# Residuals and down-product sums of two of three chunks with tokens on partitions, in a two-layer decoder step on one Trainium2 core

## The chip, the cores and the metric

One core of one Trainium2 chip runs the whole step. The metric is the time of one execution in device microseconds: for the kernel before, a median of 2242.09 us over three runs (2241.4 to 2243.4). The profiled execution is one more run, and every duration in this text comes from it. Engines are called as in the profile: PE (TensorE), DVE (VectorE), ACT (ScalarE), POOL (GpSimd), SP (which issues most DMAs).

## The reference

1088 tokens (1024 of a prompt, 64 of a sample) pass two layers. Each layer is a mixer sub-layer and an FFN sub-layer, with RMSNorm ahead of and behind each:

```python
for l in range(2):
    h = rmsnorm(x, g_mix_pre[l])
    if l == 0:   # u, xb, gate_b, gate_c = h @ w_in (1024 -> 2048)
        m = concat([pool_mixer(u), gate_b * conv3(gate_c * xb)]) @ w_out
    else:        # u, v = h @ w_uv (1024 -> 2048); v is normed, mixed over 128 positions
        m = (u * spatial(rmsnorm(v))) @ w_out_c
    x = x + rmsnorm(m, g_mix_post[l])
    h = rmsnorm(x, g_ffn_pre[l])
    f = square(relu(h @ w_up[l])) @ w_down[l]      # 1024 -> 4096 -> 1024
    x = x + rmsnorm(f, g_ffn_post[l])
```

Outputs are x for prompt and sample, the last rows of pool and convolution inputs, and the normed v of the sample.

## The kernel before

**Tiling.** The tokens are three chunks CH: 384, 384 and 320 (256 of the prompt and the 64 of the sample). Every activation lies with features on partitions: a chunk's residual X and its sums ACC are eight tiles of 128 features by n tokens. A product goes to the PE in three passes over halves in the fp32r format (`mm3`, L304): hi·hi at L308, hi·lo at L309, lo·hi at L310, with 128x128 of the weights stationary and the chunk's n tokens moving. So a product in the profile is 128x384 or 128x320; only v of the SGU (L1005) has activations stationary and 256 weight columns moving.

**Weights** (class at L30) stream from DRAM by SP into three raw buffers; ACT rounds them to the high half (L126), DVE subtracts to get the low half (L127), and eight slots hold the result. A slot comes free when its tile is done, and the next is then prepared. In the FFN's last down group the chunks come one after the other, and its weights are listed, loaded and split once for each chunk (`list_ffn`, L276).

**A down product** (`down_unit`, L483, in mixer and SGU; `products`, L953, in the FFN) makes one feature tile of 128 by n tokens; ACT copies the first group's result into ACC, DVE adds later ones (L491, L965).

**A boundary** between two sub-layers (`boundary`, L414) needs the sum over features, that is over partitions: ACT squares each tile and POOL adds the squares up (`sq_add`, L372, L377, L378), DVE transposes and reduces (`rstat`, L344, L348, L350), a small product with `fold` sums over partitions (L353), and six small operations give the reciprocal root (`rsqrt_small`, L330). Then the tiles of ACC are scaled (L424, DVE and POOL in turn), added to X with the post gain (L433), and rounded with the next gain into hh (ACT, L384) and hl (DVE, L385), while a second such sum gives RB, the factor that is multiplied in after the next products (for example L808). The new X is written to DRAM (xd) and read back (`reload_x`) before it is next needed.

**Order.** The code is written in the order of the PE's work; the boundaries are background generators. `pump` advances them between products by a count of steps (E_STEPS in the last block, U_STEPS in the next sub-layer's first products). An engine executes its instructions in the order in which they were written. Each sub-layer takes the chunks in the order 0, 1, 2. Behind a boundary come the leading products of the next sub-layer, chunk by chunk, as its h comes free (`until_ready`). PSUM has six `ps` and two `aux` banks. At the end `out_tiles` (L441) and `final` (L457) transpose x and ACC of each chunk to tokens on partitions (L453, L471) and store them; at the start `begin` (L570) transposes the input tokens (L580).

Of the kernel before, what the change touches and what calls it, by code (L numbers as in the profile page):

```python
# [15 lines left out]
P = 128  # L16
# [4 lines left out]
NC = len(CH)  # L21
PROMPT2 = 256
NSLOT = 8
E_STEPS = 1
FOLD_GAP = 6.0
U_STEPS = 7
F_STEPS = 3
G_STEPS = 3
# [5 lines left out]
class Weights:  # L34
# [18 lines left out]
    def rows(self, w, starts):  # L53
        vs = [w[r:r + P, :].rearrange("p (k n) -> p k n", k=KT) for r in starts]
        lo = self.add((4, P), [v[:, 0:4] for v in vs])
        hi = self.add((4, P), [v[:, 4:8] for v in vs])
        for p in zip(lo, hi):
            self.plan.append((4, list(p)))
# [4 lines left out]

    def down(self, w, k0, nk, m):
        v = w.rearrange("(k p) n -> p k n", p=P)[:, k0:k0 + nk, m * P:(m + 1) * P]
        ids = []
        for q in range(0, nk, 4):
            k = min(4, nk - q)
            ids += self.add((k, P), [v[:, q:q + k]])
        self.plan.append((4, ids))  # L70
# [63 lines left out]
    def done(self, piece, half=None):  # L134
        for s in range(len(piece[1])) if half is None else (half,):
            del self.tiles[piece[1][s]]
            self.prep()
# [3 lines left out]
def decoder_step(ctx: ExitStack, tc: tile.TileContext, I, O):  # L141
# [67 lines left out]
    stage = [a_pool.tile([P, 3 if c < 2 else 2, D], F32, name=f"st{c}", tag=f"acc{c}") for c in range(NC)]  # L209
# [47 lines left out]
    MIDDLE = ([("x", 4), ("hh", 4), ("hl", 4), ("x", 4), ("hh", 4), ("x", 4), ("hh", 4), ("hl", 2)],  # L257
              [[], [0], [1, 2], [3], [4], [5], [6, 7]])
    LAST = ([("x", 4), ("hh", 4), ("hl", 4), ("x", 4), ("hh", 4), ("hl", 4), ("x", 2), ("hh", 4)],
            [[], [0], [1, 2], [3], [4, 5], [6], [7]])  # L260
# [12 lines left out]
    def first_tile(units, u):  # L273
        return sum(k for _, k in units[:u])

    def list_ffn(wu, wd, plan):  # L276
        units, groups = plan
        for j in range(PLAIN):
            W.col(wu, j * P)
        for j in range(PLAIN, NFF, 2):  # L280
            W.pair(wu, j * P)
        for m in range(KT):
            W.down(wd, NFF - KEPT, KEPT, m)
        for g in groups[1:]:
            for _ in range(NC if g is groups[-1] else 1):
                for m in range(KT):
                    W.down(wd, first_tile(units, g[0]), sum(units[u][1] for u in g), m)

    list_ffn(I["w_up"][0], I["w_down"][0], MIDDLE)
# [4 lines left out]
    list_ffn(I["w_up"][1], I["w_down"][1], LAST)  # L294
# [85 lines left out]
    def pre_tile(c, m, g, ss, src=None):  # L380

        n, x, h = CH[c][1], X[c][:, m, :], H[c]
        v = x if src is None else src
        nc.scalar.activation(out=h[0][:, m, :], in_=v, func=AF.Copy, scale=gcol(g + m))  # L384
        nc.vector.scalar_tensor_tensor(out=h[1][:, m, :], in0=v, scalar=gcol(g + m),  # L385
                                       in1=h[0][:, m, :].bitcast(F32), op0=ALU.mult, op1=ALU.subtract)
        if src is not None:
            (nc.scalar.copy if m % 2 else nc.vector.tensor_copy)(out=x, in_=src)
        if ss is not None:
            sq_add(m, x, ss, n)  # L390
# [17 lines left out]

    def reload_x(c):
        n = CH[c][1]  # L410
        X[c] = x_pool.tile([P, KT, n], F32, name=f"x{c}", tag=f"x{c}")
        nc.sync.dma_start(out=X[c].rearrange("p k n -> p (k n)"), in_=xd[c])
# [28 lines left out]
    def out_tiles(c):  # L441

        n, x = CH[c][1], X[c]
        ot = h_pool.tile([P, 3 if c < 2 else 2, D], F32, name=f"ot{c}", tag=f"hl{c}")
        OT[c] = [ot[:, j] for j in range(3 if c < 2 else 2)]
        if c == 2:
            OT[c].append(w_pool.tile([P, D], F32, name="ot_s", tag="w")[0:64])
        for j, o in enumerate(OT[c]):
            r = o.shape[0]
            for g in range(2):  # L450
# [3 lines left out]
                nc.scalar.copy(out=o[:, g * 512:(g + 1) * 512], in_=ps[0:r, :])  # L454
                yield

    def final(c, ss1, gpost):  # L457
# [8 lines left out]
        for j, o in enumerate(OT[c]):  # L466
            r = o.shape[0]
            for g in range(2):
# [3 lines left out]
                oh = o[:, g * 512:(g + 1) * 512]  # L472
# [10 lines left out]
    def down_unit(c, ws, fs, first, ss1=None, steps=0):  # L483
        n, acc = CH[c][1], ACC[c]
        for m in range(KT):
            ps = psum()
            mm3(ps[:, 0:n], [W.get(p, m) + (f[:, 0, :], f[:, 1, :]) for p, f in zip(ws, fs)])
            if first:
                nc.scalar.copy(out=acc[:, m, :], in_=ps[:, 0:n])
            else:  # L490
                nc.vector.tensor_tensor(out=acc[:, m, :], in0=ps[:, 0:n], in1=acc[:, m, :], op=ALU.add)  # L491
            if ss1 is not None:
                sq_add(m, acc[:, m, :], ss1, n)
            if c == NC - 1 and m % 4 == 3:
                for p in ws:
                    W.done(p, m // 4)
            pump(steps)

# [6 lines left out]
    def spare(c, where):  # L505

        shape = [P, 2, CH[c][1]]
        if where == "h":
            return h_pool.tile(shape, F32R, name=f"fh{c}", tag=f"hh{c}")
        if c < 2:  # L510
            return a_pool.tile(shape, F32R, name=f"fa{c}", tag=f"acc{c + 1}")
        return mix_pool.tile(shape, F32R, name="fm", tag="mixa")

    def new_acc(c):
        ACC[c] = a_pool.tile([P, KT, CH[c][1]], F32, name=f"acc{c}", tag=f"acc{c}")
# [3 lines left out]
    def last_block(ws, fs, gpost, gpre, spill=False, vtok=False):  # L519

        for c in range(NC):
            ss1 = tmp()
            down_unit(c, ws, [f[c] for f in fs], False, ss1, E_STEPS if gpre is not None else F_STEPS)
            READY[c] = NORMED[c] = False
            bg.append(boundary(c, ss1, gpost, gpre, spill, vtok) if gpre is not None else final(c, ss1, gpost))

    def up_down(plan, evac, lead_in, gpost, gpre, spill, vtok, before_last=None):
        fs = {}
        for q, (kind, js) in enumerate(plan):
            ws = take(len(js))  # L530
            if kind == "U":
                pairs = list(zip(js, ws))
                spared = plan[-2][1][-1]
                if q == 0 and lead_in:
                    order = [(j, w, c) for c in range(NC) for j, w in pairs]
                else:
                    order = [(j, w, c) for j, w in pairs for c in range(NC)]
                for j, w, c in order:
                    f = None
                    if q == 0 and lead_in:  # L540
                        if j == 0:
                            while len(bg) > NC - 1 - c:
                                pump(1)
                            f = spare(c, "acc")
                    if j == spared:
                        f = spare(c, "h")
                    fs.setdefault(j, {})[c] = evac(j, c, w, f)
                    if c == NC - 1:
                        W.done(w)
                    pump(U_STEPS)  # L550
                if q == 0:
                    drain()
            elif kind == "D":
                first = js[0] == 0
                for c in range(NC):
                    if first:
                        new_acc(c)
                    down_unit(c, ws, [fs[j][c] for j in js], first)
                for j in js:
                    fs.pop(j)  # L560
            else:
                if before_last:
                    before_last()
                if gpre is None:
                    for c in range(NC):
                        bg.append(out_tiles(c))
                last_block(ws, [fs.pop(j) for j in js], gpost, gpre, spill, vtok)


    def begin(c):  # L570
# [3 lines left out]
        direct = c == 0  # L574
        if direct:
            new_h(c)
        def turn(ps, j, m):
            v = staged(c, j)[:, m * P:(m + 1) * P]
            r = v.shape[0]
            nc.tensor.transpose(ps[:, j * P:j * P + r], v, ident[0:r, 0:r])  # L580

        if direct:
            pss = [psum() if m < 6 else aux() for m in range(KT)]
            for j in range(3):
                for m in range(KT):
                    turn(pss[m], j, m)
# [571 lines left out]
```

## Time and profile before

| | |
|---|---|
| median of three runs | 2242.09 us (2241.4 to 2243.4) |
| the profiled execution's own time | 2240.17 us |
| its span, first to last instruction | 2238.4 us |
| mean granted clock of the PE | 0.982 |
| busy share of the span | PE 96%, DVE 59%, ACT 34%, POOL 10% |
| PE instructions, DVE, ACT, POOL | 13119, 2479, 1450, 229 |

The page gives busy times, 40 slices of the span, DMA queues, the chain that ended last and the costliest groups of instructions. A share over the whole span mixes stretches with different limits, so windows of single stretches, the waits of one engine and its timeline are read beside it. In a row of the timeline the first number is the start in us, the second the length, and in square brackets the idle time before it with what ended it. Starts of PE rows are measured, their ends modelled, so the distance of starts is what a product costs in a stream.

### The profile page before, as it was taken

How to read it: one execution, taken by the hardware profiler on the slowest of the kernel's cores; microseconds unless marked ns; L12 is line 12 of the kernel's file. 1: busy time of each engine (PE TensorE's matmuls, PEld its weight loads, DVE VectorE, ACT ScalarE, POOL GpSimd, SP SyncE). 2: the span in 40 equal slices, each digit the busy share in tenths (PEclk: the TensorE clock that was granted, in tenths of full speed). 3: DMA queues.
4: the chain of work that ended last, by engine and by line, in shares of the span. 5: the costliest groups of instructions: out<-in, count | busy, mean ns of one | idle time of the engine just before them, and what ended most of it. 6: DMA issues, size and time to landing. Idle time of an engine off the chain costs nothing. (4 is left out here: it accounts for less than half of the span.)

```text
span 2238.4 us, 33370 instructions
## 1 busy us (share of the span) xinstructions
PE 2149.3 (96%) x13119; PEld 2127.2 (95%) x13119; DVE 1331.0 (59%) x2479; ACT 752.6 (34%) x1450; POOL 231.7 (10%) x229
## 2 busy tenths in 40 slices
PE   7999997999999999999789999889999999999998
PEld 7999996999999999999789999879999999999997
DVE  6746677966666334445973545688666663343256
ACT  5331133533335212113442221435333361121045
POOL 3100054000000000001530000640000000000002
PEclk9999998999999999999899999989999999999999
DMA  6211222433334223225321113224333352142053
GB/s 203 84 40 49 67 96 90 137 109 98 102 106 159 62 79 107 83 78 172 111 93 57 56 41 113 67 84 137 104 106 94 106 164 89 45 129 63 28 188 121
DMA packets 252608, 219.07 MB, mean 98 GB/s; under 512 B 11744, under 2 KB 241628, under 8 KB 249372
## 3 DMA queue, kind: packets, MB, share of 16 engines
q1 hardware_dynamic: 224076, 165.11, 23.9%
q10 hardware_dynamic: 28376, 51.84, 6.5%
q8 instruction: 103, 1.69, 0.3%
q14 instruction: 53, 0.43, 0.1%
HBM read 160.74 MB, written 56.28 MB: 97 GB/s over the span
## 5 line engine op out<-in xcount | busy, mean ns | idle before, releaser
L309 PE MATMUL ps<-hl,w 128*128 128x384 f32 (+1 forms) x1696 | 559.0, 330 | 10.7 <-DVE hl L385 10.5
L308 PE MATMUL ps<-hh,w 128*128 128x384 f32 (+1 forms) x1696 | 557.0, 331 | 11.9 <-ACT hh L384 10.9
L310 PE MATMUL ps<-hh,w 128*128 128x384 f32 (+1 forms) x1696 | 557.5, 329 | 4.8 <-DVE w L127 4.8
L126 ACT CAST w<-raw 128x512 fp32r<-128x512 f32 (+1 forms) x468 | 277.5, 598 | 758.6 <-PE ps L310 686.0
L310 PE MATMUL ps<-F,w 128*128 128x384 f32 (+1 forms) x1440 | 473.3, 329 | 11.7 <-DVE w L127 11.7
L308 PE MATMUL ps<-F,w 128*128 128x384 f32 (+1 forms) x1440 | 472.9, 328 | 0.0
L309 PE MATMUL ps<-F,w 128*128 128x384 f32 (+1 forms) x1440 | 472.1, 328 | 0.0
L127 DVE TENSOR_TENSOR w<-raw,w 128x512 fp32r<-128x512 f32 (+1 forms) x468 | 317.6, 683 | 188.6 <-ACT w L126 186.6
L309 PEld LDWEIGHTS ps<-hl,w 128*128 128x128 f32 x1696 | 324.3, 191 | 16.8 <-DVE hl L385 16.7
L965 DVE TENSOR_TENSOR acc<-ps,acc 128x384 f32<-128x384 f32 (+1 forms) x288 | 152.4, 533 | 315.1 <-PE ps L310 314.9
L308 PEld LDWEIGHTS ps<-hh,w 128*128 128x128 f32 x1696 | 324.2, 192 | 13.9 <-ACT hh L384 12.2
L310 PEld LDWEIGHTS ps<-hh,w 128*128 128x128 f32 x1696 | 324.3, 191 | 5.7 <-DVE w L127 5.4
L310 PEld LDWEIGHTS ps<-F,w 128*128 128x128 f32 x1440 | 272.6, 189 | 13.0 <-DVE w L127 13.0
L378 POOL TENSOR_TENSOR tmp<-tmp 128x384 f32<-128x384 f32 (+1 forms) x105 | 108.4, 1033 | 1686.6 <-ACT tmp L377 1685.2
L308 PEld LDWEIGHTS ps<-F,w 128*128 128x128 f32 x1440 | 272.6, 189 | 0.2 <-ACT w L126 0.2
L309 PEld LDWEIGHTS ps<-F,w 128*128 128x128 f32 x1440 | 272.5, 189 | 0.0
L809 ACT ACTIVATE f<-f 128x384 f32<-128x384 f32 (+1 forms) x192 | 96.4, 506 | 178.2 <-DVE f L808 176.7
L308 PE MATMUL ps<-f,w 128*128 128x384 f32 (+1 forms) x432 | 141.3, 329 | 4.4 <-ACT f L501 4.4
L890 DVE TENSOR_TENSOR f<-ps,f 128x384 f32<-128x384 f32 x182 | 100.9, 554 | 74.3 <-PE ps L310 68.7
L310 PE MATMUL ps<-f,w 128*128 128x384 f32 (+1 forms) x432 | 141.9, 328 | 0.0
L309 PE MATMUL ps<-f,w 128*128 128x384 f32 (+1 forms) x432 | 141.6, 328 | 0.0
L309 PE MATMUL ps<-t,w 128*128 128x384 f32 x312 | 104.6, 335 | 0.0
(202 smaller groups left out, 2673.5 us busy)
## 6 DMA issues: line engine op xcount, KB each, us to landing
raw<-in_w_down_dram SPq DMA_DIRECT2D x144, 256.0 KB, 2.9
raw<-in_w_up_dram SPq DMA_DIRECT2D x128, 256.0 KB, 3.0
fd<-f ACTq DMA_DIRECT2D x120, 192.0 KB, 2.0
F<-fd SPq DMA_DIRECT2D x28, 768.0 KB, 7.2
xd<-x ACTq DMA_DIRECT2D x8, 1536.0 KB, 7.2
x<-xd SPq DMA_DIRECT2D x8, 1536.0 KB, 8.3
fd<-f ACTq DMA_DIRECT2D x60, 160.0 KB, 1.9
F<-fd SPq DMA_DIRECT2D x14, 640.0 KB, 5.2
```

What stands on the lines that cost most here:

```text
L126: nc.scalar.copy(out=wt[:, 0], in_=raw)
L127: nc.vector.tensor_tensor(out=wt[:, 1], in0=raw, in1=wt[:, 0].bitcast(F32), op=ALU.subtract)
L308: nc.tensor.matmul(out, lhsT=lh, rhs=rh, start=(j == 0), stop=False)
L309: nc.tensor.matmul(out, lhsT=lh, rhs=rl, start=False, stop=False)
L310: nc.tensor.matmul(out, lhsT=ll, rhs=rh, start=False, stop=(j == last))
L378: nc.gpsimd.tensor_tensor(out=ss[:, 0:n], in0=ss[:, 0:n], in1=t[:, 0:n], op=ALU.add)
L809: nc.scalar.activation(out=o, in_=o, func=AF.Square)
L890: tt(out=out, in0=ps, in1=v, op=ALU.add)
L965: tt(out=acc[:, m, :], in0=ps, in1=acc[:, m, :], op=ALU.add)
```

## The change

For chunks 0 and 1 the residual X and the sums ACC now have tokens on partitions: three blocks of 128 tokens by 1024 features. Chunk 2 stays with features on partitions. Each sub-layer's down products, boundary and leading products take the chunks in the order 2, 0, 1 (ORD).

- *Down products* of chunks 0 and 1 (`down_tok`) have 128 tokens of the activation stationary and 512 columns of the weights moving, so a group makes six results of 128x512 and not eight of 128x384. A down group takes both halves of the columns, each over all chunks, and its four weight tiles come free together. The last group's weights are listed once.
- *Boundaries* of chunks 0 and 1 (`boundary_tok`) sum squares along the free dimension on ACT; per block of 128 tokens DVE makes one product with reciprocal root and post gain (the gains are spread over the partitions by a DMA) and one addition over 1024 features, then ACT squares x and writes normed x into ACC (`normed`). There is no fold product and no factor RB: `plainly`, `times` and `squared` leave it out for these chunks.
- *`arrive`* transposes normed ACC of a chunk by 24 products into all eight PSUM banks, and ACT and DVE make hh and hl from there with the gain.
- X of chunks 0 and 1 starts as the input tokens and is stored at the end without transposes; `sums` (the FFN's Strassen sums) is computed from hh and hl. E_STEPS goes from 1 to 3, and x is reloaded one down group earlier in the FFN.

The core of the diff:

```diff
+ORD = (2, 0, 1)
-E_STEPS = 1
+E_STEPS = 3
...
+    def normed(c, j, v, junk, out):
+        ms = sm.tile([P, 1], F32, name="ms", tag="ms")
+        nc.scalar.activation(out=junk, in_=v, func=AF.Square, scale=1.0 / 32.0, accum_out=ms)
+        _, r = rsqrt_small(ms, 1)
+        nc.scalar.activation(out=out, in_=v, func=AF.Copy, scale=r)
...
+    def boundary_tok(c, last):
...
+        for j in range(3):
+            ms = sm.tile([P, 1], F32, name="ms", tag="ms")
+            nc.vector.tensor_tensor(out=ms, in0=SS1[c][:, j, 0:1], in1=SS1[c][:, j, 1:2], op=ALU.add)
+            _, r = rsqrt_small(ms, 1)
+            nc.vector.scalar_tensor_tensor(out=acc[:, j], in0=acc[:, j], scalar=r, in1=GB[0], op0=ALU.mult, op1=ALU.mult)
+            nc.vector.tensor_tensor(out=x[:, j], in0=x[:, j], in1=acc[:, j], op=ALU.add)
...
+            yield
+            normed(c, j, x[:, j], acc[:, j], acc[:, j])
+            nc.scalar.dma_start(out=xd[c][:, j * D:(j + 1) * D], in_=x[:, j])
+            yield
+        TOK[c] = True
+
+    def arrive(c, g):
+        while not TOK.get(c):
+            pump(1, True)
+        new_h(c)
+        n = CH[c][1]
+        pss = [psum() if m < 6 else aux() for m in range(KT)]
+        for m in range(KT):
+            for j in range(3):
+                nc.tensor.transpose(pss[m][:, j * P:(j + 1) * P], ACC[c][:, j, m * P:(m + 1) * P], ident)
+        for m in range(KT):
+            v, (hh, hl) = pss[m][:, 0:n], H[c]
+            nc.scalar.activation(out=hh[:, m, :], in_=v, func=AF.Copy, scale=gcol(g + m))
+            nc.vector.scalar_tensor_tensor(out=hl[:, m, :], in0=v, scalar=gcol(g + m),
+                                           in1=hh[:, m, :].bitcast(F32), op0=ALU.mult, op1=ALU.subtract)
+
+    def sum_tok(c, j, h, v, first, last):
+        acc = ACC[c][:, j, h * 512:(h + 1) * 512]
...
+            nc.vector.tensor_tensor(out=acc, in0=v, in1=acc, op=ALU.add)
+        if last:
+            junk = fslot(c, F32).rearrange("p a n -> p (a n)")[:, 0:512]
+            nc.scalar.activation(out=junk, in_=acc, func=AF.Square, scale=1.0 / 32.0, accum_out=SS1[c][:, j, h:h + 1])
+
+    def down_tok(c, j, h, p, right, first, last=False):
+        t = slice(j * P, (j + 1) * P)
...
+            terms.append((fh[:, t], fl[:, t], w[:, 0].rearrange("p a n -> p (a n)"), w[:, 1].rearrange("p a n -> p (a n)")))
+        mm3(ps, terms)
+        sum_tok(c, j, h, ps, first, last)
...
+    def last_block(ws, right, gpost, gpre, spill, vtok):
+        for c in ORD:
...
+            for j, h in order:
+                down_tok(c, j, h, ws[h], right[c], False, True)
+                if c == ORD[-1] and j == 2:
+                    W.done(ws[h])
+                pump(E_STEPS)
+            bg.append(boundary_tok(c, gpre is None))
...
-        for c in range(NC):
-            n, ss1 = CH[c][1], tmp()
-            for m in range(KT):
-                w = take(1)[0]
-                products(len(GROUPS) - 1, w, m, c)
-                W.done(w)
-                sq_add(m, ACC[c][:, m, :], ss1, n)
-                pump(G_STEPS)
+        last_block(take(2), unit(len(UNITS) - 1), gpost, gpre, spill, vtok)
```

The order of instructions, at the first boundary (mixer to FFN of layer 0). On PE of the kernel before, the fold product (L353) of chunk 0's second statistics stands inside the FFN's leading products of that chunk (hh_3073, hl_3074):

```order
L309 MATMUL ps<-hl_3074,w 128x384
L310 MATMUL ps<-hh_3073,w 128x384
L353 MATMUL aux<-red,fold 128x12
L308 MATMUL ps<-hh_3073,w 128x384
L309 MATMUL ps<-hl_3074,w 128x384
```

In the change the feature chunk goes first, and its second fold (L339 now) stands inside the last block, between the down products of chunk 1 (w moving, 512 columns; f and fh hold the mixer's results):

```order
L294 MATMUL ps<-w,fh_2642 128x512
L295 MATMUL ps<-w,fh_2642 128x512
L296 MATMUL ps<-w,fh_2642 128x512
L339 MATMUL aux<-red,fold 128x10
L294 MATMUL ps<-w,f_2140 128x512
```

So what waits behind this fold moved from leading products to down products.

On PE of the change, at the end of chunk 2's leading products (hh_2937) and ahead of chunk 0's (hh_3463); acc_1340 is chunk 0's normed ACC:

```order
L296 MATMUL ps<-hh_2937,w 128x320
L454 MATMUL ps<-ident,acc_1340 128x128 x5
L454 MATMUL aux<-ident,acc_1340 128x128
L454 MATMUL ps<-ident,acc_1340 128x128
L454 MATMUL aux<-ident,acc_1340 128x128
L454 MATMUL ps<-ident,acc_1340 128x128 x6
L454 MATMUL aux<-ident,acc_1340 128x128 x2
L454 MATMUL ps<-ident,acc_1340 128x128 x6
L454 MATMUL aux<-ident,acc_1340 128x128 x2
L294 MATMUL ps<-hh_3463,w 128x384
```

Twenty-four transposes, eight for each block of 128 tokens, came in between the leading products of two chunks; before, these followed each other directly.

On DVE of the kernel before, between the leading products of chunk 0 and those of chunk 1 (f_3382 is the reciprocal root spread out by a transpose, x_2815 chunk 1's residual):

```order
L357 STREAM_TRANSPOSE f_3382<-y 128x384
L424 TENSOR_TENSOR acc_991<-acc_991,f_3382 128x384 x2
L433 SCALAR_TENSOR_TENSOR x_2815<-acc_991,gains,x_2815 128x384 x3
L385 SCALAR_TENSOR_TENSOR hl_3462<-x_2815,gains,hh_3461 128x384
L424 TENSOR_TENSOR acc_991<-acc_991,f_3382 128x384
L385 SCALAR_TENSOR_TENSOR hl_3462<-x_2815,gains,hh_3461 128x384
```

On DVE of the change, from chunk 0's last block of 128 tokens (acc_1340, x_2711) to chunk 1's first (acc_1365, x_2713):

```order
L433 SCALAR_TENSOR_TENSOR acc_1340<-acc_1340,y,gb 128x1024
L434 TENSOR_TENSOR x_2711<-x_2711,acc_1340 128x1024
L431 TENSOR_TENSOR ms<-ss_3019 128x1
L322 TENSOR_SCALAR v<-ms 128x1 x2
L323 RECIPROCAL y<-y 128x1
L324 TENSOR_TENSOR t<-v,y 128x1
...
L327 TENSOR_TENSOR y<-t,y 128x1
L433 SCALAR_TENSOR_TENSOR acc_1365<-acc_1365,y,gb 128x1024
L434 TENSOR_TENSOR x_2713<-x_2713,acc_1365 128x1024
L458 SCALAR_TENSOR_TENSOR hl_3464<-ps,gains,hh_3463 128x384
```

Scales, x updates and hl by feature tile (L424, L433, L385 of before) gave way to operations over 1024 features and small ones; chunk 0's first hl (L458) now stands behind chunk 1's first block.

## Rows read from the trace of the kernel before

**Rows 1.** The page, busy time by engine: us, share of the span, instructions.
```profile
PE 2149.3 (96%) x13119; PEld 2127.2 (95%) x13119; DVE 1331.0 (59%) x2479; ACT 752.6 (34%) x1450; POOL 231.7 (10%) x229
```
**Rows 2.** The page, the chain that ended last, by engine.
```profile
PE 42%; DVE 4%; DMA 1%; issue 1%; ACT 0%; POOL 0%; DVEq 0%; ACTq 0%; SPq 0%; POOLq 0%
```
**Rows 3.** Windows: length, busy PE, PEld, DVE, ACT, POOL, clock, DMA share, GB/s.
```profile
320.00:420.00 100.00, 82.82 (x445) 78.30 (x444) 87.36 (x160) 47.33 (x101) 41.51 (x36) 0.91 0.31 105
1060.00:1160.00 100.00, 78.14 (x497) 75.24 (x496) 91.24 (x167) 47.04 (x115) 51.04 (x46) 0.90 0.34 114
1430.00:1515.00 85.00, 66.54 (x350) 62.44 (x349) 70.61 (x125) 37.37 (x80) 43.25 (x38) 0.88 0.29 99
1700.00:1800.00 100.00, 100.00 (x613) 100.00 (x612) 67.11 (x115) 38.20 (x70) 0.00 (x0) 1.00 0.31 96
```
**Rows 4.** Waits of PE: line, releaser, us in total, times, longest.
```profile
PE aux L353 <- DVE red L350: 21.2, 9, 6.0
PE ps L310 <- DVE w L127: 16.4, 7, 4.9
PE ps L308 <- ACT hh L384: 10.9, 4, 3.8
...
PE ps L308 <- ACT f L501: 4.4, 2, 2.4
```
**Rows 5.** Timeline of PE at the third boundary.
```profile
1454.63 0.57 PE L353 MATMUL aux<-red,fold 128*128 128x12 f32 x2 [5.98 <-DVE red L350]
...
1456.47 0.52 PE L309 MATMUL ps<-hl,w 128*128 128x384 f32 x1
1456.79 0.52 PE L310 MATMUL ps<-hh,w 128*128 128x384 f32 x1
```
**Rows 6.** Timeline of PE, first and last starts of unbroken stretches of one width.
```profile
1204.93 0.28 PE L308 MATMUL ps<-w,hh 128*128 128x256 f32 x1
...
1209.97 0.28 PE L308 MATMUL ps<-w,hh 128*128 128x256 f32 x1
...
1959.68 0.33 PE L308 MATMUL ps<-F,w 128*128 128x384 f32 x1
...
1965.40 0.31 PE L308 MATMUL ps<-F,w 128*128 128x320 f32 x1
...
1968.91 0.34 PE L308 MATMUL ps<-F,w 128*128 128x384 f32 x1
```
**Rows 7.** Timeline of PE, transposes at the end of the program.
```profile
2163.97 2.79 PE L453 MATMUL ps<-ident,x 128*128 128x128 f32 x12 [2.83 <-DMA x<-xd]
...
2206.39 1.03 PE L471 MATMUL ps<-ident,acc 128*128 128x128 f32 x8
```
**Rows 8.** Groups by line and shape: busy us, mean ns | idle before, releaser.
```profile
L948 DVE TENSOR_TENSOR F<-F 128x1536 fp32r<-128x1536 f32 x28 | 49.2, 1756 | 28.5 <-ACT F L947 28.4
L127 DVE TENSOR_TENSOR w<-rawsum,w 128x512 fp32r<-128x512 f32 x52 | 35.9, 691 | 4.1
L385 DVE SCALAR_TENSOR_TENSOR hl<-x,gains,hh 128x320 fp32r<-128x320 f32 x32 | 27.2, 860 | 0.0
L433 DVE SCALAR_TENSOR_TENSOR x<-acc,gains,x 128x320 f32<-128x320 f32 x24 | 18.4, 794 | 0.0
L424 DVE TENSOR_TENSOR acc<-acc,f 128x320 f32<-128x320 f32 x12 | 7.9, 679 | 0.0
```
**Rows 9.** Groups by line and shape: small operations of the reciprocal root.
```profile
L338 DVE TENSOR_TENSOR t<-v,y 128x12 f32<-128x12 f32 x16 | 3.3, 206 | 0.4
L335 ACT ACTIVATE y<-aux,eps_t 128x12 f32<-128x12 f32 x16 | 4.3, 269 | 20.9 <-PE aux L353 20.8
```
**Rows 10.** Timeline of PE, the last product of the program.
```profile
2221.80 0.31 PE L310 MATMUL ps<-F,w 128*128 128x320 f32 x1
```
**Rows 11.** DMA issues of the last 14 us: count, KB each, median us to landing.
```profile
out_dram<-ot SPq DMA_DIRECT2D x9, 256.0 KB, 2.4
```

More of the change, by code (lines that the diff above doesn't have):

```diff
@@ L132, in get, with tile, done @@
         return t[:, 0, k % per, :], t[:, 1, k % per, :]
[L134 to L137, printed above, removed]
+    def tile(self, piece, k):
+        return self.tiles[piece[1][k]]
+    def done(self, piece):
+        for i in piece[1]:
+            self.free(i)
 @with_exitstack
@@ L271, in list_plan, with first_tile, list_ffn @@
                 W.rows(wd, [j * P for j in ts_])
[L273 to L277, printed above, removed]
+    def first_tile(u):
+        return sum(k for _, k in UNITS[:u])
+    def list_ffn(wu, wd):
         for j in range(PLAIN):
@@ L281, in list_ffn @@
             W.pair(wu, j * P)
-        for m in range(KT):
[L283 to L289, printed above, removed]
+        W.rows(wd, [k * P for k in range(NFF - KEPT, NFF)])
+        for u, (_, k) in enumerate(UNITS):
+            W.rows(wd, [(first_tile(u) + q) * P for q in range(k)])
+    list_ffn(I["w_up"][0], I["w_down"][0])
     for cb in range(4):
@@ new lines, in down_feat @@
+    def down_feat(c, m, p, right, first, ss1=None):
+        n, acc = CH[c][1], ACC[c]
+        ps = psum()[:, 0:n]
+        terms = []
+        for k, (fh, fl) in enumerate(right):
+            w = W.tile(p, k)
+            terms.append((w[:, 0, m % 4, :], w[:, 1, m % 4, :], fh, fl))
+        mm3(ps, terms)
+        if first:
+            nc.scalar.copy(out=acc[:, m, :], in_=ps)
+        else:
+            nc.vector.tensor_tensor(out=acc[:, m, :], in0=ps, in1=acc[:, m, :], op=ALU.add)
+        if ss1 is not None:
+            sq_add(m, acc[:, m, :], ss1, n)
@@ new lines, in down_group @@
+    def down_group(ws, right, first, after=None):
+        for h in range(2):
+            for c in ORD:
+                if first and h == 0:
+                    new_acc(c)
+                if c == 2:
+                    for m in range(4 * h, 4 * h + 4):
+                        down_feat(c, m, ws[h], right[c], first)
+                else:
+                    for j in range(3):
+                        down_tok(c, j, h, ws[h], right[c], first)
+                if h and after:
+                    after(c)
+            W.done(ws[h])
@@ L481, in final @@
                 yield
[L483 to L497, printed above, removed]
     def split_f(c, src, f=None):
@@ L517, in decoder_step, with rights @@
     fd = [dram.tile([P, NFF, n], F32, name=f"fd{c}") for c, (off, n) in enumerate(CH)]
[L519 to L527 removed]
+    def rights(fs):
+        return {c: [(f[c][:, 0, :], f[c][:, 1, :]) for f in fs] for c in range(NC)}
@@ L1000, in decoder_step @@
+        for u in range(-1, len(UNITS) - 1):
+            load(u + 1)
+            if u == len(UNITS) - 2:
+                for c in ORD:
+                    reload_x(c)
+            down_group(take(2), unit(u), u < 0, lambda c: split(u + 1, c))
+        post_gain("g_ffn_post", layer)
+        if gpre is None:
+            bg.append(out_tiles(2))
+        last_block(take(2), unit(len(UNITS) - 1), gpost, gpre, spill, vtok)
     ffn(0, G_MIX_PRE + 8, True, True)
```

380 lines of the change are left out of this document (178 added, 202 removed).

## Prediction

> **What bounds the kernel now.** I read the page first: TensorE (PE) is busy 96% of the span, VectorE (DVE) 59% [rows 1]; the chain that ended last is PE by far, with DVE next at 4% [rows 2]. So the time is the PE's stream plus the places where it breaks. The windows show where [rows 3]. In a steady stretch of the FFN the PE is busy 100.00 of 100 us at clock 1.00; what the other engines do there costs nothing. At the three boundaries where norms must be finished before the next products (mixer to FFN 320–420, FFN to SGU 1060–1160, SGU to FFN 1430–1515) the PE is busy 82.82 of 100, 78.14 of 100 and 66.54 of 85 us, at clocks 0.91, 0.90 and 0.88. Idle time plus what the clock takes (length times one minus the clock) is 17.2 + 9.0 = 26, 21.9 + 10 = 32 and 18.5 + 10.2 = 29 us: **87 us in all**. Next, who is waited for [rows 4]: the fold product of the statistics waits for DVE (21.2 us), products for a split weight tile (16.4), for the first normed tiles hh (10.9), and for a split FFN activation f (4.4). What follows a wait is slow too: after the wait of 5.98 at 1454.63 products of 384 columns start 0.32 us apart, against 0.173 in the steady stretch; that is the 1.2 GHz level after idling [rows 5, 6].
>
> **The change, part by part.** The sum is made against the profiled execution, 2240.2 us (span 2238.4 and 1.8 outside it); the median of the runs shown is 1.9 above that, and I add it at the end. About 4.5 us (0.2%) is what a measurement here can tell from no change.
>
> 1. *Wide down products.* For two chunks 3840 products of 384 columns become 2880 of 512: the same columns, 960 fewer products. In unbroken stretches 33 products of 384 take 5.72 us, 24 of 320 take 3.51 and 42 of 256 take 5.04 [rows 6], i.e. 173.3, 146.3 and 120.0 ns each. All three are columns/2.4 GHz + 13.3 ns, so 512 should take 226.7, and each product that goes saves 13.3 ns: **−12.8 us**. The bound on the poor side is no saving (512 at 4/3 of 173.3 = 231.1). The products of 256 already have activations stationary and weights moving, so that exchange costs nothing by itself. The Trainium skill, TensorE: Matmul & The Clock Gate, section "Wait — 56ns, not 53.3ns?", gives a fixed cost of about 2.5 ns per warm product, not 13.3; by it this term would be an estimated −2.4 us. The three pitches here disagree with it, and the trace decides.
>
> 2. *Transposes.* Three boundaries get 2 × 24 each (+144); 96 at the output go. Eight in the stream took 1.03 us, about 0.107 each without the tail that the model adds to the last; twelve after a wait took 2.79, about 0.21 each [rows 7]. 48 × 0.107 = **+5 us**; with all new ones at the slow level 144 × 0.21 − 96 × 0.107 = +20. I keep +5, since the first sixteen of an arrival can run in time that the PE would idle. The Trainium skill, same page, "Part 4: PE-mode transpose", says that the fast clock does not engage for transposes, which would be the +20; the eight at 0.107 speak against it.
>
> 3. *Boundaries.* What goes for two chunks: a scale, an update of x and an hl from SBUF per feature tile, each 0.68 to 0.86 us on DVE even at 320 columns [rows 8], and the POOL sums behind the folds. What comes: per 128 tokens two DVE operations of 1024 and some fourteen small ones, two ACT passes of 1024, later hl from PSUM. A two-input operation of 1024 is not in the trace: two of 512 are 1.38, two thirds of 1536 is 1.17, and the line between 0.691 and 1.756 gives 1.22 [rows 8]. I take that for ACT's passes too. Small operations take 0.2 in a dependent row, the square root 0.27 [rows 9].
> The order, with time from the token chunks' first last-block unit: twelve units of 12 products of 512, 2.72 us each, 32.6. The feature chunk's first fold stands behind the fourth unit (10.9), its second behind the tenth (27.2), but between them DVE has 4 scales of 0.679, 8 updates of 0.794, 8 hl of 0.860, five sums of 0.69 and 2.7 of small operations, transpose and reduce: 22.1. So the second fold can run at 33.0, and a **wait of 5.8 us stays there**; two more go to the clock after it. The units end at 40.4. The feature chunk's leading products, 96 × 0.146 = 14.0, cover to 54.4. The squares of the token chunks want an f slot that the mixer's and SGU's operands hold until the last unit, so chunk 0's chain starts at about 40. Per 128 tokens it is 0.2 + 0.27 + 1.2 and 2 × 1.22 (post norm and x), 1.22 (square), 0.27 + 1.2 and 1.22 (copy): 8.0, three times 24, ready at 64.4. The PE idles about 10, and the last transposes, first evictions and slow level cost about 3 over the two arrivals. That is 5.8 + 2 + 10 + 3 = **21 us lost per boundary** whose operands sit in f slots, and some 18 at the FFN-to-SGU one, which has no such slots, and where most of the waits for weight tiles (16.4 us in seven [rows 4]) fall: the last down group's weights are now prepared once (8 tiles) and not once per chunk. 87 falls to 60: **−27 us**. The bounds: 12 per boundary (chains that overlap) is −51; no gain at all is 0.
>
> 4. *FFN hand-over.* The two waits for f behind the up products (4.4 in two [rows 4]) go, since the feature chunk's first four units of two terms (24 × 0.146 = 3.5 us) now cover the split of chunk 0's last tile: **−5 us** with the slow level after them; uncovered, 0.
>
> 5. *Start and end.* Chunks 0 and 1 are normed before they are transposed, so the first products come later, but no wait for their statistics follows, and DVE and POOL have less to do in the first mixer phase: **−1.5**, between +4 and −5. At the end x is reloaded one group earlier, so the wait of 2.83 goes [rows 7], −3. Behind the last product, ended at about 2222.1 of 2238.4 [rows 10], that is 16.3 us, stand now a sum (0.7), a square (0.8), two chains of 1.5 + 2.4 in row on DVE and a store of 512 KB, between one and two times the 2.4 of 256 KB [rows 11]: 11.7 to 14.1. I take 14.3 with hand-overs, **−2**, together −5.
>
> 6. *At nothing:* sums into ACC (6 of 512 for 8 of 384) lie beside a PE at 100% with DVE at 67% [rows 3]; without that cover they would move a few tenths per group. POOL loses most of its work, off the chain. SP issues the gains' broadcast ahead of the twelve units, which it has to land; the reloads of x now stand ahead of weight tiles one group earlier, and what is late next if they hold these up is the group before the last. Weight slots come free four at once and not one: hidden by half a group, 23 us, against 4 tiles of 0.69 on DVE.
>
> Sum: −12.8 + 5 − 27 − 5 − 1.5 − 5 = −46.3, so 2193.9 in a profiled run and **2196 us** as a median.
>
> **Rivals.** *Boundaries don't gain* (term 3 zero): the wait for chunk 0's chain takes the place of the waits for folds, hh and weights. For it: DVE stays busiest there, and the chain changes between ACT and DVE four times per 128 tokens. Against: less DVE work in all, and 14 us of cover. Time 2196 + 27 = **2223**.
> *Slower:* chunk 0's chain is stretched because its small DVE operations each stand behind other DVE work (weight splits, relu of the feature chunk, chunk 1's chain): at 0.69 behind every one of some forty the 24 us become 52, the idle 38 and not 10 at each boundary. That is +84, so **2280**; it decides from 17 us more per boundary on (46.3 + 4.5, by three). Against it: in the DVE order chunk 1's first multiply stands behind chunk 0's third.
> *Wide products save nothing* (231.1 each): 2196 + 12.8 = **2209**. For it: no product of 512 is in the trace. Against: three pitches on one line. The Trainium skill's rule in term 1 would land close by.
> That the change doesn't do what it says is excluded by the order of instructions: PE has 928 fewer matmuls, POOL 138 fewer operations.
>
> **How the numbers follow.** Forecast 0.60, its own range 2170 to 2207; boundaries without gain 0.20; wide products without gain 0.10; slower 0.10. The first three are faster by over 0.2% but for a tail of the second, 0.03; so faster 0.87, same 0.03, slower 0.10. Range: 2170 (boundaries at 12 each) to 2232 (the second rival with the start at its bad end); outside are the slower case and a little below.
>
> **What would show it.** In the profile after: products of 512 columns 0.227 apart in the steady FFN; a PE wait of 5 to 6 us at a boundary's second fold; then a PE idle of 8 to 11 us ahead of the last transposes of chunk 0, named as waiting for ACT's normed copy; dips of the clock at the same three places, shallower; no wait for f or x. I am wrong if chunk 0's arrival idles the PE for over 16 us, if wide products stand 0.231 or more apart, or if waits for weight tiles appear in the steady FFN.

## The result and the profile after

The changed kernel takes 2180.41 us (median of 4 runs, 2178.21 to 2182.16), the kernel before 2242.74 (4 runs): a ratio of 0.9722, interval 0.9705 to 0.9738, so 62 us less. The profiled execution has a span of 2177.0 us against 2238.4.

Of the page, busy time by engine and the chain that ended last, which answer to [rows 1, 2]:

```profile
PE 2113.6 (97%) x12175; PEld 1985.4 (91%) x12175; DVE 1275.7 (59%) x2521; ACT 689.5 (32%) x1302; POOL 73.0 (3%) x93
...
PE 91%; DVE 6%; DMA 1%; ACT 1%; issue 1%; SPq 0%; POOL 0%; ACTq 0%; DVEq 0%; POOLq 0%
```

The chain of before is followed back only to 1180 us, which is why its shares in [rows 2] add up to 48%; its 42% and the 91% here can't be set against each other.

The same windows as [rows 3], moved with the shorter program, the second one 15 us longer (three boundaries, a steady stretch of the FFN):

```profile
300.00:400.00 100.00, 88.66 (x476) 81.88 (x475) 81.71 (x203) 57.02 (x122) 11.88 (x11) 0.93 0.30 103
1050.00:1165.00 115.00, 103.85 (x717) 96.80 (x716) 76.66 (x202) 57.72 (x144) 12.42 (x13) 0.94 0.25 87
1390.00:1475.00 85.00, 73.55 (x403) 68.09 (x402) 70.69 (x178) 53.93 (x116) 11.06 (x11) 0.92 0.33 115
1600.00:1700.00 100.00, 100.00 (x611) 100.00 (x610) 67.55 (x116) 29.65 (x51) 0.00 (x0) 1.00 0.33 102
```

The three boundaries still dip, less than before; POOL's 41 to 51 us there are down to 11 or 12. The PE's waits, against [rows 4]:

```profile
PE ps L454 <- ACT acc L417: 18.6, 9, 4.2
PE aux L339 <- DVE red L336: 14.7, 3, 5.1
...
PE ps L294 <- DVE hl L458: 5.7, 7, 3.3
```

Nothing waits for weight tiles or x any more, and f stands at 0.6 us. Two waits are left at every boundary: the second fold (L339), and the transposes (L454) for a chunk's normed copy (L417). Of the latter's 18.6 us, 15.5 lie at the boundaries and 3.1 at the start of the program.

**Where the 61.4 us of span went.** I set each stretch of the PE against what its products would take at columns/2.4 GHz + 13.3 ns, and call the rest lost. The boundary rows cover 320 to 420, 1060 to 1200 and 1430 to 1515 us before and the first three windows above after; a single row holds to within 1 us, since a stretch can be cut in more than one place. The starts of all products, stretch by stretch, give:

| stretch | lost before | lost after | forecast of the difference |
|---|---|---|---|
| start (0–100) | 28.7 | 27.6 | −1.5 |
| mixer to FFN | 29.1 | 19.9 | −5 |
| up to down products, twice | 6.5 | 0.9 | −5 |
| FFN to SGU | 37.6 | 20.4 | −14 |
| SGU to FFN | 29.8 | 19.0 | −8 |
| end | 22.4 | 15.4 | −5 |
| elsewhere | 13.2 | 13.3 | 0 |
| sum | 167.3 | 116.5 | −38.5 |
| the products themselves | 2071.1 | 2060.5 | −7.8 |

### The profile page after: what moved, and what is told of

The parts are those of the page before. It is cut to its first block, busy times and chain, and to the rows that moved or that the text cites. A ratio compares the mean times of both kernels' runs of the same rounds, so it can differ in the third digit from the quotient of the medians.

```text
span 2177.0 us, 30946 instructions
## 1 busy us (share of the span) xinstructions
PE 2113.6 (97%) x12175; PEld 1985.4 (91%) x12175; DVE 1275.7 (59%) x2521; ACT 689.5 (32%) x1302; POOL 73.0 (3%) x93
## 4 chain that ended last, share of the span: by engine, by line
PE 91%; DVE 6%; DMA 1%; ACT 1%; issue 1%; SPq 0%; POOL 0%; ACTq 0%; DVEq 0%; POOLq 0%
PE ps L294 30%; PE ps L296 30%; PE ps L295 30%; DVE hl L370 1%; DVE x L554 1%; DVE acc L467 1%; PE aux L1157 1%; DVE x L434 1%; DVE acc L433 1%; DMA x<-in_x_prompt_dram 1%; DVE w L117 0%; DVE acc L545 0%; DVE hl L458 0%; DMA F<-fd 0%; DMA raw<-in_w_down_dram 0%
## 5 line engine op out<-in xcount | busy, mean ns | idle before, releaser
L295 PE MATMUL ps<-hl,w 128*128 128x384 f32 (+1 forms) x1696 | 550.1, 325 | 0.1
L116 ACT CAST w<-raw 128x512 fp32r<-128x512 f32 x404 | 248.9, 621 | 649.3 <-PE ps L296 572.8
L117 DVE TENSOR_TENSOR w<-raw,w 128x512 fp32r<-128x512 f32 x404 | 275.2, 688 | 147.8 <-ACT w L116 144.1
L467 DVE TENSOR_TENSOR acc<-ps,acc 128x512 f32<-128x512 f32 x240 | 164.7, 688 | 263.3 <-PE ps L296 263.2
L294 PE MATMUL ps<-w,F 128*128 128x512 f32 x720 | 281.7, 391 | 0.0
L296 PE MATMUL ps<-w,F 128*128 128x512 f32 x720 | 281.3, 391 | 0.0
L295 PE MATMUL ps<-w,F 128*128 128x512 f32 x720 | 281.2, 391 | 0.0
L296 PEld LDWEIGHTS ps<-w,F 128*128 128x128 f32 x720 | 135.7, 189 | 28.6
L295 PEld LDWEIGHTS ps<-w,F 128*128 128x128 f32 x720 | 135.7, 189 | 27.2
L294 PEld LDWEIGHTS ps<-w,F 128*128 128x128 f32 x720 | 135.7, 189 | 27.1
L294 PE MATMUL ps<-F,w 128*128 128x320 f32 x480 | 148.3, 309 | 0.0
L296 PE MATMUL ps<-F,w 128*128 128x320 f32 x480 | 148.3, 309 | 0.0
L295 PE MATMUL ps<-F,w 128*128 128x320 f32 x480 | 148.3, 309 | 0.0
L493 DVE TENSOR_TENSOR acc<-ps,acc 128x320 f32<-128x320 f32 x160 | 76.9, 489 | 105.2 <-PE ps L296 104.1
L1029 ACT CAST F<-F 128x1536 fp32r<-128x1536 f32 (+3 forms) x48 | 64.1, 1335 | 206.4 <-DMA F<-fd 198.1
```

What stands on the lines that cost most here:

```text
L116: nc.scalar.copy(out=wt[:, 0], in_=raw)
L117: nc.vector.tensor_tensor(out=wt[:, 1], in0=raw, in1=wt[:, 0].bitcast(F32), op=ALU.subtract)
L294: nc.tensor.matmul(out, lhsT=lh, rhs=rh, start=(j == 0), stop=False)
L295: nc.tensor.matmul(out, lhsT=lh, rhs=rl, start=False, stop=False)
L296: nc.tensor.matmul(out, lhsT=ll, rhs=rh, start=False, stop=(j == last))
L467: nc.vector.tensor_tensor(out=acc, in0=v, in1=acc, op=ALU.add)
```

## The experiments

Each was timed in three rounds beside the kernel before; ratios are to that kernel, and the change stands at 0.9722 (0.9705 to 0.9738).

**1. Narrow products again.** In `down_tok`:

```diff
-        mm3(ps, terms)
+        for q in range(2):
+            s = slice(q * 256, q * 256 + 256)
+            mm3(ps[:, s], [(fh_, fl_, wh[:, s], wl[:, s]) for fh_, fl_, wh, wl in terms])
```

> The changed kernel, but each down product of 512 weight columns is made as two of 256: the same columns, 2880 more products. Theory (13.3 ns for each product on top of its columns): 2880 x 13.3 ns = 38 us more than the change, about 2219 us, and products of 256 start 0.120 us apart. Rival A (a fixed 2.5 ns for each product): 7 us more, about 2188. Rival B (columns alone count, and the gain of the change came from the boundaries): no difference, 2180.

Measured: 2212.89 us, ratio 0.9876 (0.986 to 0.9893); the span is 2211.7, 34.7 more than the change's. Timelines of the PE in steady down products: of the change (the first of 72 wide products, and what follows the last), then of the experiment (144 of 256):

```profile
1931.68 0.39 PE L294 MATMUL ps<-w,F 128*128 128x512 f32 x1
...
1948.02 0.30 PE L294 MATMUL ps<-F,w 128*128 128x320 f32 x1
```

```profile
1933.40 0.28 PE L294 MATMUL ps<-w,F 128*128 128x256 f32 x1
...
1950.67 0.31 PE L294 MATMUL ps<-F,w 128*128 128x320 f32 x1
```

That is 16.34 / 72 = 226.9 ns and 17.27 / 144 = 119.9 ns, both on the line from [rows 6] (226.7 and 120.0). The products account for 38 us more, and some 3 less are lost, most of it in the waits for the fold (11.3 us and not 14.7): a unit of 24 narrow products takes 2.88 us and not 2.72, so DVE has more time up to the fold. The theory stands, and with it the sign and size of term 1: the 960 products that went are worth 12.8 us. The Trainium skill's 2.5 ns (TensorE: Matmul & The Clock Gate, "Wait — 56ns, not 53.3ns?") would have made this experiment an estimated 7 us; with these fp32r products it was 35.

**2. The second fold later.** `rstat` of the second statistics yields a gap of 14.0 us and not FOLD_GAP, so the fold product stands behind the last block:

```diff
-        yield FOLD_GAP
+        yield gap
```

> The changed kernel, but the fold product of the feature chunk's second statistics is written 14 us of PE work behind its reduce and not 6, so behind the last block. Theory (the three waits of 4.8 to 5.1 us on it are lost time, with the slow clock after them): they go, 14 to 20 us less than the change, 2161 to 2167. Rival (the waits lie ahead of work that is not ready anyway): the waits for chunk 0's normed tiles grow by as much, and the time stays within 3 us of 2180.

Measured: 2174.31 us, ratio 0.9704 (0.969 to 0.9719). Waits of PE, and its timeline at the first boundary:

```profile
PE ps L454 <- ACT acc L417: 26.9, 12, 3.9
...
342.73 1.28 PE L454 MATMUL ps<-ident,acc 128*128 128x128 f32 x6 [2.49 <-ACT acc L417]
...
348.33 1.54 PE L454 MATMUL ps<-ident,acc 128*128 128x128 f32 x6 [3.89 <-ACT acc L417]
...
353.72 1.54 PE L454 MATMUL ps<-ident,acc 128*128 128x128 f32 x6 [3.42 <-ACT acc L417]
```

All three waits for the fold are gone, but those for the normed tiles grew from 18.6 to 26.9: of 14.7 us some 6 are kept by median, under 5 in the spans (2172.4), 4 by the ratios, whose intervals just overlap. Neither forecast holds; the truth lies nearer the rival: what ends a boundary is chunk 0's chain.

**3. A tile of its own for the squares.** In `sum_tok`:

```diff
-            junk = fslot(c, F32).rearrange("p a n -> p (a n)")[:, 0:512]
+            junk = JUNK[0]
```

> The changed kernel, but the squares of the token chunks' sums have a tile of their own for their unused output and do not wait for an f slot. Theory of the prediction (chunk 0's chain starts late because its squares wait for slots held by mixer and SGU operands): the chain starts some 8 us earlier at those two boundaries, the waits for normed tiles there (5.8 us each) go, 8 to 14 us less, 2166 to 2172. Rival (the chain starts late because its first multiply stands in DVE's order behind the sum of chunk 1's last unit): squares come earlier, the multiply does not, and the time stays within 3 us of 2180.

Measured: 2179.72 us, ratio 0.9732 (0.9718 to 0.9747): no difference from the change. DVE of the experiment at the first boundary, chunk 1's last sum and chunk 0's first multiply:

```profile
333.84 0.69 DVE L468 TENSOR_TENSOR acc<-ps,acc 128x512 f32<-128x512 f32 x1 [0.27 <-PE ps L296]
...
336.58 1.28 DVE L434 SCALAR_TENSOR_TENSOR acc<-acc,y,gb 128x1024 f32<-128x1024 f32 x1
```

Chunk 0's squares ran from 297.34 on and not from 307.44 as in the change, and yet its first multiply came at 336.58 (334.68 in the change), still behind chunk 1's last sum. My reason for the late chain was wrong in this order of work, though its time was right.

**4. The last down group's weights three times.** `list_ffn` lists the last unit once for each chunk again, and `last_block` takes and releases two pieces per chunk:

```diff
-            W.rows(wd, [(first_tile(u) + q) * P for q in range(k)])
+            for _ in range(NC if u == len(UNITS) - 1 else 1):
+                W.rows(wd, [(first_tile(u) + q) * P for q in range(k)])
```

> The changed kernel, but the weights of the FFN's last down group are loaded and split once for each chunk, as before the change. Theory (the boundary from FFN to SGU gained 17 us and the two others 9 and 11 because the repeated weights went): 6 to 10 us more at that boundary, and 0 to 4 at the end of the program, 2186 to 2194, with waits for weight tiles in both places. Rival (the repeated weights cost nothing, the larger gain has another reason): within 3 us of 2180.

Measured: 2180.56 us, ratio 0.9733 (0.9719 to 0.9748). The rival holds: at the FFN-to-SGU boundary two waits for weights appear (2.1 and 1.9 us), the wait for the fold there goes, and the sum is nothing; at the end of the program no wait for weights appears. In the new layout the single loading, which I gave a part of the FFN-to-SGU gain, is worth nothing.

**5. The pace of before.** E_STEPS = 1 in the changed kernel.

> The changed kernel, but the background work of a boundary is advanced by one step behind each product unit of the last block, as before the change, and not by three. Theory (the gain came from layout, not from the pace): the second fold then falls behind the last block as in the run with the late fold, and chunk 0's chain starts behind it, so 2172 to 2184. Rival (the pace gave much of the gain): 2195 or more, with waits for the feature chunk's own tiles.

Measured: 2189.75 us, ratio 0.9777 (0.9762 to 0.9791), between the two. The wait of PE for the normed copies, and its last rows:

```profile
PE ps L454 <- ACT acc L417: 34.7, 13, 6.1
```

```profile
2159.82 0.39 PE L296 MATMUL ps<-w,F 128*128 128x512 f32 x1
...
2160.19 2.82 PE L591 MATMUL ps<-ident,acc 128*128 128x128 f32 x24
```

As in 2 the second fold falls behind the last block and costs nothing, and the wait for chunk 0 grows in its place. Counted by starts, the three boundaries lose 19.8, 20.5 and 19.5 us, as much as in the change. What is lost more lies at the end: the last product starts 4 us earlier than in the change (2163.76), but the span goes on for 27.7 us behind that start, and for 13.2 in the change. Behind it stand the feature chunk's 24 output transposes and the last operations of all six token blocks; in the change three blocks are left. So some 9 to 12 of the change's 62 us hang on the pace of three, and they lie at the end of the program, not at the boundaries.

**6. The pace of three in the kernel before**, and one step instead of three in its FFN's last down group:

> The kernel before, with three background steps behind each unit of the mixer's and SGU's last block (one before) and one behind each of the FFN's last down group (three before). Theory (the FFN-to-SGU boundary lost most before because its background work stood ahead of weight splits in DVE's order, pumped three times a unit): there some 6 to 12 us less, and the pace of three at the two others gives up to 9 us each way: 2222 to 2240 in all. Rival (the weight splits alone, three times over, were the cause): the waits for weight tiles at that boundary stay at 11 to 16 us.

Measured: 2241.18 us (2235.84 to 2247.78), ratio 1.0003 (0.9992 to 1.0015). The profiled execution is the longest of the ten, so its single stretches are read with care. Waits of PE between 1060 and 1180, of the kernel before, then of the experiment:

```profile
PE ps L310 <- DVE w L127: 11.7, 5, 4.9
...
PE ps L309 <- DVE w L127: 3.3, 2, 2.2
```

```profile
PE ps L310 <- DVE hl L385: 5.7, 7, 1.4
PE ps L308 <- ACT hh L384: 5.3, 1, 5.3
PE ps L310 <- DVE w L127: 5.0, 4, 2.6
...
PE ps L308 <- ACT w L126: 2.3, 1, 2.3
```

The waits for weight tiles fell from 15.0 us to 7.3 in this boundary, so the rival fails, and waits for hl and hh took their place: the stretch lost 41 us of PE time and not 37.6 in this execution, and the whole gained nothing. The old layout does not profit from another order of its DVE work.

**7. Turns.** With the late fold and the own tile of 2 and 3, the boundaries of the feature chunk and the token chunks advance alternately, each with its own gap, in four steps per unit, and the token chain in finer steps (a step ends after the square, and after the root). The queue's core:

```diff
+            n = 1
+            if bg[0][2]:
+                while n < len(bg) and bg[n][2]:
+                    n += 1
+            pick = [i for i in range(n) if force or pe[0] >= bg[i][1]]
...
+            e = bg.pop(pick[0])
...
+                bg.insert(n - 1, e)
```

> The changed kernel with the late second fold and a tile of its own for the squares, and the background work of the feature chunk's and the token chunks' boundaries taken in turns, the token chunks' in finer steps. Theory (chunk 0's chain comes late because it stands behind the feature chunk's boundary and behind the last unit's sums in the order of DVE and ACT): the chain starts some 20 us earlier, the waits for chunk 0's normed tiles (18.6 us, 26.9 with the late fold) fall under 6, with less slow clock: 2148 to 2160. Rival (DVE's amount of work in a boundary is the bound, whatever its order): the waits move to the feature chunk's tiles and the time stays within 6 us of the run with the late fold, 2168 to 2180.

Measured: 2161.62 us, ratio 0.9654 (0.9639 to 0.9668), faster than the change. DVE's row of chunk 0's first multiply at the first boundary, then PE's waits and two windows (the first two boundaries):

```profile
306.11 1.25 DVE L455 SCALAR_TENSOR_TENSOR acc<-acc,y,gb 128x1024 f32<-128x1024 f32 x1
```


```profile
PE aux L352 <- DVE red L349: 6.2, 3, 2.1
PE ps L307 <- DVE hl L480: 5.0, 4, 3.3
PE aux L476 <- ACT acc L439: 4.1, 4, 1.3
...
300.00:400.00 100.00, 93.42 (x520) 86.45 (x519) 89.55 (x218) 58.64 (x123) 13.16 (x11) 0.98 0.31 105
1050.00:1165.00 115.00, 106.48 (x778) 100.16 (x778) 76.14 (x190) 56.77 (x145) 14.26 (x13) 0.99 0.24 82
```

The chain starts 29 us earlier than in the change (334.68), and its second block 11 us earlier. At the boundaries the waits for the token chunks' normed copies fell from 15.5 us to 4.7 (4.1 and a rest of 0.6), and the granted clock of the two windows rose from 0.93 and 0.94 to 0.98 and 0.99: with shorter waits, spread out, little time at the lower level is left. The theory is right on the cause; 2161.6 is just above its range. The run changes several things at once: turns, finer steps and four steps per unit are not told apart here (9 tells the tile apart). This and the versions in 8 and 9 are clearly faster than both kernels.

**8. Turns with the fold at 20 us**, then also with six steps.

> The kernel with turns, the second fold 20 us of PE work behind its reduce and not 14. Theory: its three waits of 2.1 us go, 4 to 7 us less than with turns, 2155 to 2158. Rival (the feature chunk's first evictions, which need that statistic, fill the PSUM banks and stop the PE instead): 2161 or more.

> The kernel with turns and 20 us, with six background steps behind each unit and not four. Theory (the chain of chunk 0 is no longer what ends last): within 4 us of the one with four steps. Rival (still late): 5 to 10 less.

Measured: 2161.28 us, ratio 0.9644 (0.963 to 0.9659), and 2162.34, ratio 0.9649 (0.9634 to 0.9663): the same as turns. With 20 us no fold is waited for, but weight tiles are:

```profile
PE ps L309 <- DVE w L117: 6.2, 3, 2.9
...
PE ps L308 <- DVE w L117: 3.6, 2, 3.1
```

The three waits became others of DVE: the time is the rival's, but the waits are not those that it named. Six steps give nothing more, so chunk 0's chain is no longer what ends last.

**9. Turns with the squares in f slots again.**

> The kernel with turns, but the squares of the token chunks write into f slots again, as in the change. Theory (the slots did not matter in the change because the chain stood behind other work; with turns the squares of chunk 0 come at its last unit and the chain starts there anyway): 0 to 4 us more than with turns, 2161 to 2166. Rival of the prediction (the slots hold the chain up once nothing else does): 8 or more us more, from the two boundaries whose operands sit in f slots, 2170 or more.

Measured: 2167.71 us, ratio 0.9674 (0.966 to 0.9689), 6 us more than turns, between the two. Chunk 0's first multiply at the first boundary:

```profile
326.50 1.28 DVE L454 SCALAR_TENSOR_TENSOR acc<-acc,y,gb 128x1024 f32<-128x1024 f32 x1
```

It came at 306.11 with a tile of its own. So the slots do hold the chain up, once the order of work no longer does. Against the late fold alone (2174.31) this run has only turns, finer steps and four steps per unit: these are worth 6.6 us, and the tile another 6.

**10. The order 0, 2, 1** of the chunks, at three steps and at two.

```diff
-ORD = (2, 0, 1)
+ORD = (0, 2, 1)
```

> The changed kernel with the chunks in the order 0, 2, 1 in place of 2, 0, 1. Theory (what counts is the time between a token chunk's last down product and its transposes): chunk 0's chain lies under 30 us of the other chunks' down products, so its waits go, and of the boundary's 20 us some 5 to 10 go: 2150 to 2166; what is late next is chunk 0's hl behind the feature chunk's x and hl in DVE's order. Rival (a feature chunk ahead is needed as cover): 2180 or more.

> As the order 0, 2, 1, with two background steps behind each unit and not three. Theory: less of the feature chunk's x and hl stands ahead of chunk 0's hl on DVE, 0 to 8 us less than with three. Rival (chunk 0's chain is then too slow): up to 8 more.

Measured: 2195.42 us, ratio 0.9803 (0.9788 to 0.9818), and 2182.32, ratio 0.9743 (0.9726 to 0.9759). Waits of PE with three steps:

```profile
PE ps L294 <- DVE hl L458: 29.0, 5, 9.8
PE ps L454 <- DVE acc L467: 13.0, 3, 5.2
PE ps L454 <- ACT acc L417: 9.4, 5, 2.8
```

The wait for chunk 0's normed copies shrank as expected, but what I had named as late next weighs more: chunk 0's hl stands on DVE behind the feature chunk's x and hl (at the first boundary its first row comes at 344.34, 10 us behind the first transposes at 334.08). The transposes even wait for the last sums (L467), since they need all eight PSUM banks. Two steps get 13 us back, so the rival's claim is not shown: with two steps the boundaries lose about as much as in the change, 3 us more are lost at the end, and the intervals of the two ratios overlap.

## Why the prediction was right, and where its sizes failed

The forecast of a gain was right, 2180.4 lies within 2170 to 2232, and the loss left at the boundaries came out as worked out, in sum. The size was 46 us where 62 came. In the spans it was short by 15 us: 10 are term 3, 3 are the products and transposes (terms 1 and 2), 2 are the end.

- **Term 1** (wide products, −12.8) is confirmed by the pitch of 226.9 ns and by experiment 1.
- **Term 2** (+5). In a stream twelve transposes take 1.46 us up to the next, 0.12 each; after a wait of 4.19 us six take 1.34, so 0.22. The granted clock, the last but two of a window's numbers, was 1.00 at the former and 0.50 at the latter:

```profile
1127.44 1.62 PE L454 MATMUL ps<-ident,acc 128*128 128x128 f32 x12
1128.90 0.60 PE L454 MATMUL aux<-ident,acc 128*128 128x128 f32 x4
1129.75 0.88 PE L454 MATMUL ps<-ident,acc 128*128 128x128 f32 x6 [0.25 <-ACT acc L417]
...
355.43 1.54 PE L454 MATMUL ps<-ident,acc 128*128 128x128 f32 x6 [4.19 <-ACT acc L417]
356.77 0.63 PE L454 MATMUL aux<-ident,acc 128*128 128x128 f32 x2
```

```profile
1127.40:1129.70 2.30, 2.10 (x18) 1.69 (x16) 0.80 (x4) 1.60 (x3) 0.00 (x0) 1.00 0.00 2
355.40:357.40 2.00, 1.97 (x8) 1.57 (x8) 1.97 (x3) 1.46 (x4) 0.00 (x0) 0.50 0.00 0
```

  Both prices of the prediction hold. The faster one, at a clock of 1.00, speaks against what term 2 quotes from the Trainium skill (TensorE: Matmul & The Clock Gate, "Part 4: PE-mode transpose"), that the fast clock does not engage for transposes. At the products' law 48 more transposes are 3.2; what they take beyond that stands in the lost time.
- **Term 3, the failed size.** Lost after: forecast 60 us (21, 18, 21), measured 59.3 (19.9, 20.4, 19.0). The fold's wait is 4.75, 5.09 and 4.85 (forecast 5.8); leading products end 54.7 us after the token chunks' first unit (54.4), chunk 0 is ready at 62.8 (64.4), its three blocks take 20.8 (24). The chain's start at 42 (40) was right for the wrong reason: not the f slots, but its place behind the fold and behind chunk 1's last sums in DVE's and ACT's order (experiments 3 and 7); the slots become the limit only once that order is changed (9). The sum of 60 was met in part by luck. Ahead of chunk 0's transposes the PE idles 5.8, 3.9 and 5.8 us, not the 8 to 11 that were named as a sign (the longest such wait of the first boundary is the 4.19 in the row above), and slow starts and short pauses take 7.5 to 9 us at each boundary, for which 5 were counted. What failed is the other end of the subtraction, the step "87 us in all". Idle time plus clock misses what the PE loses in pauses shorter than the modelled rest of a product: a row of 0.33 us covers a start that comes 0.15 late, where starts should stand 0.173 apart. This hid some 6 us. And the window to 1160 left out 3.3 us of slow starts up to 1200. By starts the three boundaries lost 29.1 + 37.6 + 29.8 = 96.5 before. By idle and clock the change's windows would have 18.3, 18.1 and 18.3, that is 54.7 for the true 59.3. So the term is −37, not −27.
- **Terms 4 and 5.** The hand-over gave −5.6 (−5). The start gave −1.1 (−1.5), no more than the 1 us within which a row holds: the first product came at 22.01, not 14.38, and later waits went. The end gave −7.0 (−5), and it hangs on the pace of three (experiment 5), of which the prediction says nothing. The last product ended at 2164.15, read as in [rows 10], 12.8 us from the end of the span (14.3):

```profile
2163.76 0.39 PE L296 MATMUL ps<-w,F 128*128 128x512 f32 x1
```

- **The rivals.** "Boundaries don't gain": they gained 37 us. "Slower" needed a chain of 40 us: it takes 21, but with another order of the work the boundaries lose 18 us less (experiment 7, with the late fold and the own tile) or 11 us more (10). "Wide products save nothing": excluded by experiment 1. The upper end of the range, 2232, is more than its terms give: 2223 with the start at +4 and not −1.5 is 2228.5.
- **Open.** Why FFN to SGU gained 17 us and the others 9 and 11. Not the repeated weights, as far as the new layout can show it (experiment 4), nor the pace (6). That DVE was fullest there before, 91.24 of 100 us with POOL at 51.04 [rows 3], fits and was not tried by itself. How the 37 us of the boundaries divide among less work on DVE, faster operations without POOL beside them, and fewer waits for folds and weights was not separated either.

## What to carry to other kernels

Take the time lost in a stretch from the starts of its products against their pitch, not from idle time: short pauses hide under modelled ends, and here they were 7 to 8% of a boundary's loss. When a boundary is bound by a chain of one tile through two in-order engines, look first at what stands ahead of its first link on each; taking turns in finer steps was worth 6.6 us, and with the late fold and the tile for the squares 15 to 19, while freeing the slot that it seemed to wait for gave nothing until that was done and 6 us then. See where in the program a run loses its time before naming a cause: one step for three cost nothing at the boundaries that it was aimed at, and 9 to 12 us at the end. A single wait that is taken away gives back only what the next one in that chain leaves.

## What the runs showed of the hardware that was not expected

DVE operations of one form come in two durations. DVE and then POOL of the change, at the first boundary:

```profile
311.69 0.54 DVE L554 SCALAR_TENSOR_TENSOR x<-acc,gains,x 128x320 f32<-128x320 f32 x1
...
316.87 1.16 DVE L554 SCALAR_TENSOR_TENSOR x<-acc,gains,x 128x320 f32<-128x320 f32 x1
317.95 1.16 DVE L370 SCALAR_TENSOR_TENSOR hl<-x,gains,hh 128x320 fp32r<-128x320 f32 x1
319.04 0.68 DVE L467 TENSOR_TENSOR acc<-ps,acc 128x512 f32<-128x512 f32 x1
...
323.41 0.68 DVE L467 TENSOR_TENSOR acc<-ps,acc 128x512 f32<-128x512 f32 x1
```

```profile
306.11 4.44 POOL L545 TENSOR_TENSOR acc<-acc,f 128x320 f32<-128x320 f32 x4 [11.17 <-DVE f L343]
313.03 5.73 POOL L364 TENSOR_TENSOR f<-f,tmp 128x320 f32<-128x320 f32 x5 [2.48 <-ACT tmp L363]
319.13 0.88 POOL L364 TENSOR_TENSOR f<-f,tmp 128x320 f32<-128x320 f32 x1 [0.36 <-ACT tmp L363]
```

With both inputs in SBUF they take 0.54 us while POOL rests (310.55 to 313.03) and 1.16 while POOL adds; a sum with one input in PSUM takes 0.68 either way. The means of 0.79 and 0.86 in [rows 8] were a mixture of the two: of the 56 operations of these two groups, the 15 with no POOL operation beside them took 0.53 to 0.55 us each. So a layout that takes work from POOL also makes DVE faster, which no step of the prediction counted. The Trainium skill, GPSIMD Engine Reference, "1. Specifications", says that GpSimd shares its SBUF interfaces with VectorE and contends with instructions of two SBUF inputs; the rows agree.
